# A two-layer encoder on one core: the next layer's loads issued behind operand loads of w_ffn_out, and PSUM buffers of its own for the last of seven products

## The chip, the cores and the metric

The kernel runs on one core of one Trainium2 chip. The metric is the device time of one launch in microseconds. Before the change three runs took 2110.39, 2110.87 and 2112.12 us; the median is 2110.87.

The engines are called by their names in the profile: PE (TensorE, matrix products into PSUM), PEld (its weight loads), DVE (VectorE), ACT (ScalarE), POOL (GpSimd) and SP (SyncE, whose queue issues nearly all DMAs of this kernel). Each runs its own instructions in order and waits for others by semaphores.

## The reference

Two layers over x of 1024 tokens by 1024 channels, all float32:

```python
for l in range(DEPTH):                                    # DEPTH = 2
    h = _rmsnorm(x, g_pre_mix[l])
    z = h @ w_in[l]
    zf, zq, zk, zv, zm = jnp.split(z, splits, axis=-1)
    y_f = _fourier_mix(zf, w_fourier[l])
    ...                                                   # y_a: windowed attention of zq, zk, zv
    mkv = _rmsnorm(mem, g_mem[l]) @ w_mem_kv[l]           # mem: 256 rows by 1024
    km, vm = jnp.split(mkv, 2, axis=-1)
    y_m = _memory_attn(zm.reshape(b, s, N_MEM_HEADS, HEAD_DIM), km, vm)
    ...                                                   # x = x + norm(concat(y_f, y_a, y_m) @ w_out[l])
    ...                                                   # gate, up = norm(x) @ w_ffn_in[l]; width 2816 each
    ...                                                   # x = x + norm((silu(gate) * up) @ w_ffn_out[l])
```

The memory projection `mkv` depends on inputs alone, so the kernel can make that of layer 1 at any time while layer 0 runs.

## The kernel before, in words

**Precision.** Every matrix product of float32 operands is made as three products of high and low halves: `split` (ACT L151 copies the high half, DVE L152 subtracts it to get the low half) makes `hi` and `lo`, and PE adds hi x hi, hi x lo and lo x hi.

**Stages.** A layer is mixing (projections, Fourier, windowed and memory attention, output projection), then `ffn_in` (product with w_ffn_in, silu and gate), then `ffn_out` (product with w_ffn_out). Both parts of the FFN work by Strassen's scheme: of each matrix cut into two by two quarters, seven products of sums of quarters instead of eight. `ffn_in` writes the seven sums of gated quarters to DRAM (`actd`, L1193), 11 tiles of 128 x 512 for each product.

**`ffn_out`** (L1255) runs the products in the order 5, 3, 4, 1, 7, 2, 6. A product has 11 steps k. For each, `out_sums` (L1229) loads a tile of `actd` (L1233) and splits it, loads one or two blocks of w_ffn_out (L1239), adds or subtracts these on DVE (L1251) and splits the result. Then `step` (L1270) issues three matmuls of 128x128 by 128x512 for each of four row blocks p: 12 a step, 132 a product. The raw tiles live in rings of 3 (`ras`) and 6 (`rbs`) buffers, the split operands in a ring `abs_` of 6 buffers in layer 0 and 15 in layer 1. The last product of layer 1 (`late`) runs row blocks 0 and 1 over all k first, and blocks 2 and 3 after them.

**PSUM.** The four results of a product (`fo`) are in four PSUM tags `pd`, `av`, `sc`, `pT`, with two buffers each, which they share with everything else on PE. Products 5, 4, 1 and 2 take new buffers. Products 3, 7 and 6 add to the PSUM tiles of the product ahead of them (`new` is false), so that the first matmul of 6 on a tile follows the reading of product 2's result from it (L1307). After each product its tiles are added to the four quarters of the output, `c11` to `c22`, by ACT copies or DVE TENSOR_TENSORs (L1293 to L1309).

**The next layer's loads.** In layer 0, `after(i)` (L1446) is called behind each product. Behind product 5 it emits `mem.make()` for layer 1: two loads of `mem` rows (L427, 512 KB each), g_mem (L216), eight loads of w_mem_kv (L356, 256 KB each) with their splits, the transposes `mTp` on PE (L439), and the products `kmp` and `vmp` (L162; 192 matmuls in all), which take PSUM buffers of tag `pT`. Behind product 1 it emits `zf_load()` and `fourier_tables(28)`: loads of parts of w_in for layer 1 (L356, L372), scaled by a gain on POOL (L342) or on ACT and DVE (L380) and split, and small Fourier tables (L498, L501). The rest of layer 1's beginning (`hTp`, `kvp`, `zT` on PE) mixes with products 2 and 6.

**Order.** The program is written in the order of the code, and the Tile scheduler then puts each engine's instructions in an order of its own by a simulated timeline: loads that wait for nothing may go far ahead of where they are written. `tc.issue_after(x)` is a scope whose DMAs stay behind the instruction x in that order; before, only the loads of the residual `x1d` (L1426) use it, with `lastld[0]`, the `actd` load that was written last.

Of the kernel before, what the change touches and what calls it, by code (L numbers as in the profile page):

```python
# [16 lines left out]
ALU = mybir.AluOpType  # L17
# [51 lines left out]
def tile_encoder(ctx: ExitStack, tc: tile.TileContext, T, C, out):  # L69
# [36 lines left out]
    def big(*shape, dt=F32R):  # L106

        return bp.tile([P, *shape], dt, tag="big", name=nm("big"))
# [34 lines left out]
    def ps(shape, name="ps", tag="pd"):  # L143
        return psp[tag].tile([P] + list(shape), F32, tag=tag, name=nm(name))
# [24 lines left out]
    def cst(*shape):  # L169
# [20 lines left out]
        out=mask[:, 0:P], in_=mask[:, 0:P], pattern=[[1, P]], compare_op=ALU.is_ge,  # L190
# [4 lines left out]
        out=mask[:, 2 * P : 3 * P], in_=mask[:, 2 * P : 3 * P], pattern=[[-1, P]],  # L195
# [988 lines left out]
    def up_out(q, g, actd, p):  # L1184

        V, G = nc.vector, nc.vector if p == NFF // 2 - 1 else nc.gpsimd
        a = [acts(512) for _ in range(4)]
        for i, c in enumerate(q.out):
            (G if i in (0, 3) else V).tensor_tensor(out=a[i], in0=c, in1=g[i], op=ALU.mult)  # L1189
        a11, a21, a12, a22 = a  # L1190

        def put(i, s):
            nc.sync.dma_start(actd[i - 1, p], s)  # L1193

        put(3, a11)
        put(4, a22)
        for i, x, y, eng in ((1, a11, a22, G), (2, a21, a22, V), (5, a11, a12, G)):
            s = acts(512)
            eng.tensor_tensor(out=s, in0=x, in1=y, op=ALU.add)
            put(i, s)  # L1200
        V.tensor_tensor(out=a21, in0=a11, in1=a21, op=ALU.subtract)
        put(6, a21)
        G.tensor_tensor(out=a12, in0=a12, in1=a22, op=ALU.subtract)
        put(7, a12)
# [22 lines left out]
    lastld = [None]  # L1227

    def out_sums(l, actd, i, k):  # L1229

        ab = abs_(2, 2, 512, dt=F32R)
        raw = ras(512)
        lastld[0] = nc.sync.dma_start(raw, actd[i - 1, k])  # L1233
        split(ab[:, 0, 0], ab[:, 0, 1], raw)

        def block(r, c):
            w = rbs(512)
            r0 = (2 * k + r) * P
            nc.sync.dma_start(w, T["w_ffn_out"][l, r0 : r0 + P, c * 512 : c * 512 + 512])  # L1239
            return w  # L1240

        if i in (2, 5):
            s = block(i == 5, i == 5)
        else:
            x, y, op = {
                4: ((1, 0), (0, 0), ALU.subtract), 3: ((0, 1), (1, 1), ALU.subtract), 1: ((0, 0), (1, 1), ALU.add),
                7: ((1, 0), (1, 1), ALU.add), 6: ((0, 0), (0, 1), ALU.add),
            }[i]
            x, y = block(*x), block(*y)
            s = bsums(512)  # L1250
            nc.vector.tensor_tensor(out=s, in0=x, in1=y, op=op)  # L1251
        split(ab[:, 1, 0], ab[:, 1, 1], s)
        return ab

    def ffn_out(l, actd, load, out, after, half, late):  # L1255

        n = NFF // 2  # L1260
        fb = [big(2, D, dt=F32) for _ in range(4)]
        rows = [fb[t // 2][:, t % 2] for t in range(NT)]
        c11, c12, c21, c22 = ([rows[4 * r + p][:, c * 512 : c * 512 + 512] for p in range(4)] for r in range(2) for c in range(2))
        add, sub = ALU.add, ALU.subtract
        TT = nc.vector.tensor_tensor

        def step(pt, p, ab, first, last, new):
            sl = slice(p * P, p * P + P)
            for j, (x, y) in enumerate(((0, 0), (0, 1), (1, 0))):
                mm(pt, ab[:, 0, x, sl], ab[:, 1, y], start=new and first and j == 0, stop=last and j == 2, skip_group_check=not new)  # L1270

        for i in (5, 3, 4, 1, 7, 2, 6):
            new = i in (5, 4, 1, 2)
            if new:
                pts = [ps([512], "fo", ("pd", "av", "sc", "pT")[p]) for p in range(4)]
            whole = 2 if i == 6 and late else 4
            ops = []
            for k in range(n):
                ops.append(out_sums(l, actd, i, k))
                for p in range(whole):  # L1280
                    step(pts[p], p, ops[k], k == 0, k == n - 1, new)
                t = {(2, 2): 0, (2, 7): 1, (6, 1): 2, (6, 5): 3}.get((i, k))
                if t is not None:
                    load(t)
                    out(t, rows[t])
                if i == 6 and k in (7, 8, 9, 10):
                    load(k - 3)
            for p in range(4):
                pt = pts[p]
                if p >= whole:  # L1290
                    for k in range(n):
                        step(pt, p, ops[k], k == 0, k == n - 1, new)
                if i == 5:  # L1293
                    nc.scalar.copy(c22[p], pt)
                    nc.scalar.copy(c11[p], pt)
                if i == 3:
                    nc.scalar.copy(c12[p], pt)
                    TT(out=c22[p], in0=pt, in1=c22[p], op=sub)
                if i == 4:
                    nc.scalar.copy(c21[p], pt)  # L1300
                    TT(out=c11[p], in0=c21[p], in1=c11[p], op=sub)
                if i == 1:
                    TT(out=c22[p], in0=pt, in1=c22[p], op=add)
                if i == 7:
                    TT(out=c11[p], in0=pt, in1=c11[p], op=add)
                if i == 2:
                    TT(out=c21[p], in0=pt, in1=c21[p], op=add)  # L1307
                if i == 6:
                    TT(out=c22[p], in0=c22[p], in1=pt, op=sub)  # L1309
                    if late:  # L1310
                        out(4 + p, rows[4 + p])
            after(i)
        if not late:
            for t in range(4, NT):
                out(t, rows[t])
                if t == 5:
                    half()
# [25 lines left out]
    mem = Memory(0, 32, 80, 20, 16, "pd")  # L1343
    mix = Mix(0, hT, mem)
# [13 lines left out]
    for l in range(DEPTH):  # L1358
# [58 lines left out]
        if l + 1 < DEPTH:  # L1417
            mem = Memory(l + 1, 16, 0, 16, 28, "pT")
            mix = Mix(l + 1, nhT, mem)
# [26 lines left out]
        def after(i):  # L1446
            if last:
                return
            if i == 5:
                mem.make()  # L1450
            if i == 1:
                mix.zf_load()
                mix.fourier_tables(28)

        xs_.i, xs_.ks = 0, (36, 24, 12, 16, 20, 28, 0) if last else (36, 24, 28, 20, 36, 24, 28, 46)
        ffn_out(l, actd, last_x, last_tile, after, lambda: mix.zf(0), last)
        if not last:
            norm_T(st.pop(NT - 1), nhT, NT - 1, "av")
# [43 lines left out]
```

## Time and profile before

| what | us |
|---|---|
| median of three runs | 2110.87 |
| the profiled execution | 2111.43 |
| its span | 2109.6 |
| mean granted clock of PE in it | 0.978 |
| layer 0, `ffn_out`, first to last matmul | 829.09 to 1075.8 |
| layer 1, `ffn_out`, first to last matmul | 1875.04 to 2101.1 |

The span is the profiled part of the execution. The lines of the profile are read like this: a row of the timeline has a start, a length, engine, line, operation and tiles; a bracket gives the idle time of the engine ahead of it and the instruction whose end released it. "x12" counts instructions that stand together. A row's matmuls overlap, so their length is that of the row and not twelve times a mean. All that the argument needs is shown where it is used.

### The profile page before, as it was taken

How to read it: one execution, taken by the hardware profiler on the slowest of the kernel's cores; microseconds unless marked ns; L12 is line 12 of the kernel's file. 1: busy time of each engine (PE TensorE's matmuls, PEld its weight loads, DVE VectorE, ACT ScalarE, POOL GpSimd, SP SyncE). 2: the span in 40 equal slices, each digit the busy share in tenths (PEclk: the TensorE clock that was granted, in tenths of full speed). 3: DMA queues.
4: the chain of work that ended last, by engine and by line, in shares of the span. 5: the costliest groups of instructions: out<-in, count | busy, mean ns of one | idle time of the engine just before them, and what ended most of it. 6: DMA issues, size and time to landing. Idle time of an engine off the chain costs nothing.

```text
span 2109.6 us, 28534 instructions
## 1 busy us (share of the span) xinstructions
PE 2004.4 (95%) x9587; PEld 1650.9 (78%) x9587; DVE 1576.5 (75%) x2532; ACT 1068.9 (51%) x2270; POOL 715.0 (34%) x819
## 2 busy tenths in 40 slices
PE   7998999799999999999999979997999999999997
PEld 6876887588888887788788758775788888878885
DVE  5668757887877877686856786679887787778774
ACT  7467767643333334444545676776333333345441
POOL 5345436343434334100523544453342343400021
PEclk9999999899999999999999989998999999999998
DMA  6112123423323326787821112233232232379872
GB/s 218 42 51 66 69 92 116 144 75 104 111 95 108 107 86 224 279 280 262 285 92 44 45 65 86 78 133 115 85 130 95 95 110 95 112 234 332 298 270 102
DMA packets 173347, 286.48 MB, mean 136 GB/s; under 512 B 15464, under 2 KB 73360, under 8 KB 173200
## 3 DMA queue, kind: packets, MB, share of 16 engines
q1 hardware_dynamic: 165136, 265.78, 37.7%
q10 hardware_dynamic: 8064, 18.88, 2.3%
q8 instruction: 75, 1.23, 0.2%
q14 instruction: 72, 0.59, 0.1%
HBM read 218.02 MB, written 66.58 MB: 135 GB/s over the span
## 4 chain that ended last, share of the span: by engine, by line
PE 77%; DVE 7%; DMA 6%; ACT 5%; issue 3%; POOL 2%; SPq 0%; DVEq 0%; ACTq 0%; POOLq 0%
PE fo L1270 15%; PE qz L1137 10%; PE qy L1137 10%; PE qx L1137 10%; PE mo L162 7%; PE qw L1137 5%; PE kvp L162 4%; DVE arena_r L152 3%; PE qp L162 3%; PE zT L162 2%; DMA arena_f<-actd 2%; PE pT L798 2%; PE sc L761 2%; ACT arena_r L151 1%; DMA arena_f<-in_w_ffn_out 1%
## 5 line engine op out<-in xcount | busy, mean ns | idle before, releaser
L151 ACT CAST arena_r<-arena_f 128x512 fp32r<-128x512 f32 (+2 forms) x780 | 443.8, 591 | 653.6 <-PE qz L1137 116.4
L152 DVE TENSOR_TENSOR arena_r<-arena_f,arena_r 128x512 fp32r<-128x512 f32 (+1 forms) x676 | 506.8, 770 | 154.4 <-ACT arena_r L151 151.6
L1270 PE MATMUL fo<-arena_r 128*128 128x512 f32 x1848 | 433.7, 396 | 22.8 <-ACT arena_r L151 12.7
L1270 PEld LDWEIGHTS fo<-arena_r 128*128 128x128 f32 x1848 | 351.7, 191 | 100.2 <-ACT arena_r L151 15.0
L1137 PE MATMUL qy<-arena_r 128*128 128x512 f32 x1056 | 263.6, 399 | 20.6 <-ACT arena_r L151 12.4
L1137 PEld LDWEIGHTS qy<-arena_r 128*128 128x128 f32 x1056 | 202.7, 193 | 65.6 <-ACT arena_r L151 13.0
L1127 DVE TENSOR_TENSOR arena_f<-arena_f 128x512 f32<-128x512 f32 x220 | 205.8, 939 | 8.9 <-issue 2.4
L1137 PE MATMUL qz<-arena_r 128*128 128x512 f32 x704 | 196.6, 389 | 1.2 <-DVE arena_r L152 1.2
L1157 POOL TENSOR_TENSOR arena_f<-arena_f 128x512 f32<-128x512 f32 x44 | 74.3, 1688 | 311.2 <-ACT arena_f L1142 311.2
L1137 PEld LDWEIGHTS qz<-arena_r 128*128 128x128 f32 x704 | 132.1, 188 | 29.0 <-DVE arena_r L152 1.6
L210 POOL TENSOR_SCALAR rrsv<-rss 128x1 f32<-128x1 f32 x32 | 13.1, 410 | 396.8 <-ACT arena_f L323 218.1
L152 POOL TENSOR_TENSOR arena_r<-arena_f,arena_r 128x256 fp32r<-128x256 f32 (+2 forms) x104 | 85.1, 823 | 129.6 <-ACT arena_r L151 100.5
L1137 PE MATMUL qx<-big,arena_r 128*128 128x512 f32 x528 | 127.1, 389 | 1.7 <-ACT arena_f L1142 1.7
L1137 PE MATMUL qx<-arena_r 128*128 128x512 f32 x528 | 127.9, 389 | 0.5 <-ACT arena_r L151 0.5
L1137 PE MATMUL qw<-arena_r 128*128 128x512 f32 x528 | 128.3, 389 | 0.0
L1189 POOL TENSOR_TENSOR arena_f<-arena_f 128x512 f32<-128x512 f32 x40 | 66.7, 1667 | 159.7 <-DVE arena_f L1169 122.4
L1137 PEld LDWEIGHTS qx<-big,arena_r 128*128 128x128 f32 x528 | 99.0, 188 | 22.6 <-ACT arena_f L1142 2.1
L1137 PEld LDWEIGHTS qx<-arena_r 128*128 128x128 f32 x528 | 99.1, 188 | 21.4 <-ACT arena_r L151 0.9
L1137 PE MATMUL qz<-big,arena_r 128*128 128x512 f32 x352 | 115.6, 389 | 0.0
L1137 PEld LDWEIGHTS qw<-arena_r 128*128 128x128 f32 x528 | 99.1, 188 | 20.7
L162 PE MATMUL mo<-big,arena_r 128*128 128x512 f32 x384 | 102.7, 408 | 0.5 <-ACT arena_f L1001 0.5
L162 PE MATMUL mo<-arena_r 128*128 128x512 f32 x384 | 101.9, 403 | 0.5 <-ACT arena_f L1001 0.5
(227 smaller groups left out, 3516.1 us busy)
## 6 DMA issues: line engine op xcount, KB each, us to landing
arena_f<-in_w_ffn_out SPq DMA_DIRECT2D x264, 256.0 KB, 4.3
arena_f<-in_w_ffn_in SPq DMA_DIRECT2D x88, 512.0 KB, 3.7
actd<-arena_f SPq DMA_DIRECT2D x154, 256.0 KB, 3.7
arena_f<-actd SPq DMA_DIRECT2D x154, 256.0 KB, 4.1
arena_f<-in_w_in SPq DMA_DIRECT2D x40, 256.0 KB, 2.8
arena_f<-in_x SPq DMA_DIRECT2D x16, 512.0 KB, 5.3
arena_f<-in_w_out SPq DMA_DIRECT2D x32, 256.0 KB, 2.7
pmd<-arena_f ACTq DMA_DIRECT2D x32, 256.0 KB, 2.0
```

The costliest lines, as they stand in the source:

```text
L151: nc.scalar.copy(hi, src)
L152: return (lo_eng or nc.vector).tensor_tensor(out=lo, in0=src, in1=f32(hi), op=ALU.subtract)
L162: mm(self.dst, a, b, start=self.i == 0, stop=self.i == self.n - 1)
L210: nc.gpsimd.tensor_scalar(out=v, in0=ss, scalar1=1.0 / n, scalar2=EPS, op0=ALU.mult, op1=ALU.add)
L761: mm(pt, lhs, self.kst[g][i][:, k0 * P : k1 * P], start=i == 0, stop=i == 1)
L798: nc.tensor.transpose(pT[:, h, :], es_[h // 2][:, h % 2, j * P : j * P + P], ident)
L1127: nc.vector.tensor_tensor(out=s, in0=a, in1=b, op=op)
L1137: mm(pt, a, b, start=start and n == 0, stop=n == 11, skip_group_check=not start)
L1157: nc.gpsimd.tensor_tensor(out=self.v, in0=self.v, in1=self.s2, op=ALU.add)
L1189: (G if i in (0, 3) else V).tensor_tensor(out=a[i], in0=c, in1=g[i], op=ALU.mult)
L1270: mm(pt, ab[:, 0, x, sl], ab[:, 1, y], start=new and first and j == 0, stop=last and j == 2, skip_group_check=not new)
```

## The change

The loads of `after(i)` stand in an `issue_after` scope behind the last `actd` load of product i, and the memory projection moves from behind product 5 to behind product 3. Product 6 takes new PSUM buffers, as products 5, 4, 1 and 2 do. Since product 6 no longer adds to product 2's result, that result is added to `c21` and also subtracted from `c22` when product 2 ends (four more TENSOR_TENSORs a layer, L1308 after), and product 6 is added to `c22` with the sign of its operand turned (L1201).

```diff
-        V.tensor_tensor(out=a21, in0=a11, in1=a21, op=ALU.subtract)
+        V.tensor_tensor(out=a21, in0=a21, in1=a11, op=ALU.subtract)
         put(6, a21)
...
         for i in (5, 3, 4, 1, 7, 2, 6):
-            new = i in (5, 4, 1, 2)
+            new = i not in (3, 7)
             if new:
                 pts = [ps([512], "fo", ("pd", "av", "sc", "pT")[p]) for p in range(4)]
...
                 if i == 2:
                     TT(out=c21[p], in0=pt, in1=c21[p], op=add)
+                    TT(out=c22[p], in0=c22[p], in1=pt, op=sub)
                 if i == 6:
-                    TT(out=c22[p], in0=c22[p], in1=pt, op=sub)
+                    TT(out=c22[p], in0=pt, in1=c22[p], op=add)
...
         def after(i):
             if last:
                 return
-            if i == 5:
-                mem.make()
-            if i == 1:
-                mix.zf_load()
-                mix.fourier_tables(28)
+            with tc.issue_after(lastld[0].ins):
+                if i == 3:
+                    mem.make()
+                if i == 1:
+                    mix.zf_load()
+                    mix.fourier_tables(28)
```

The scheduler turns this into another order on every engine. From L1308 on, lines after are one higher than before, and from L1450 on two.

**SP, first operand loads of product 5 in layer 0**, before: between the loads of `actd` and w_ffn_out stand pieces of w_mem_kv and w_in.

```order
L356 DMA arena_f<-in_w_mem_kv 128x2x256
L1239 DMA arena_f<-in_w_ffn_out 128x512
L356 DMA arena_f<-in_w_mem_kv 128x2x256
L1233 DMA arena_f<-actd 128x512
L1239 DMA arena_f<-in_w_ffn_out 128x512 x2
L1233 DMA arena_f<-actd 128x512
L356 DMA arena_f<-in_w_in 128x2x256
L356 DMA arena_f<-in_w_mem_kv 128x2x256
L356 DMA arena_f<-in_w_in 128x2x256
L1233 DMA arena_f<-actd 128x512
```

After, the same loads begin behind the last `actd` load of product 3 (the second of the x2 in the first row here).

```order
L1233 DMA arena_f<-actd 128x512 x2
L427 DMA arena_f<-in_mem 128x1024 x2
L356 DMA arena_f<-in_w_mem_kv 128x4x128 x3
L216 DMA arena_f<-in_g_mem 128x1024
L1233 DMA arena_f<-actd 128x512 x2
L1239 DMA arena_f<-in_w_ffn_out 128x512 x3
L1233 DMA arena_f<-actd 128x512
L1239 DMA arena_f<-in_w_ffn_out 128x512 x3
L356 DMA arena_f<-in_w_mem_kv 128x4x128
```

The rest of w_mem_kv follows among product 4's loads, and the pieces of w_in stand behind the last `actd` load of product 1.

**PE, where the memory projection stands in layer 0.** After, fo_7032 to fo_7035 are products 5 and 3, and fo_7644 to fo_7647 product 4. The first rows are the end of product 3 and the start of product 4:

```order
L1270 MATMUL fo_7034<-arena_r 128x512 x3
L1270 MATMUL fo_7035<-arena_r 128x512 x3
L439 MATMUL mTp_7504<-const,arena_f 128x128 x4
L439 MATMUL mTp_7511<-const,arena_f 128x128 x4
L1270 MATMUL fo_7644<-arena_r 128x512 x3
L1270 MATMUL fo_7645<-arena_r 128x512 x3
```

and these are the projection and what follows it in product 4:

```order
L162 MATMUL kmp_7539<-arena_r 128x256 x23
L162 MATMUL kmp_7565<-arena_r 128x256 x24
L162 MATMUL vmp_7591<-arena_r 128x256 x24
L162 MATMUL vmp_7617<-arena_r 128x256 x24
L1270 MATMUL fo_7647<-arena_r 128x512 x18
L1270 MATMUL fo_7644<-arena_r 128x512
```

Before, mTp stood in the last steps of product 5 and the first of product 3, and kmp and vmp behind that; now they stand behind product 3 and inside product 4, whose fourth row block (fo_7647) makes up its first six steps, 18 matmuls, after vmp.

**DVE, the step from product 2 to product 6 in layer 0.** Before, the eviction of product 2 (L1307) mixes with operand sums (L1251) and splits (L152) of product 6 and work of layer 1:

```order
L152 TENSOR_TENSOR arena_r<-arena_f,arena_r 128x512
L1307 TENSOR_TENSOR big_7030<-fo_8376,big_7030 128x512
L1251 TENSOR_TENSOR arena_f<-arena_f 128x512
L152 TENSOR_TENSOR arena_r<-arena_f,arena_r 128x512
L1307 TENSOR_TENSOR big_7030<-fo_8377,big_7030 128x512
L1251 TENSOR_TENSOR arena_f<-arena_f 128x512
L1307 TENSOR_TENSOR big_7031<-fo_8378,big_7031 128x512
```

After, each L1307 has an L1308 behind it that reads the same PSUM tile:

```order
L152 TENSOR_TENSOR arena_r<-arena_f,arena_r 128x512
L1307 TENSOR_TENSOR big_7030<-fo_8376,big_7030 128x512
L1308 TENSOR_TENSOR big_7030<-big_7030,fo_8376 128x512
L1251 TENSOR_TENSOR arena_f<-arena_f 128x512
L152 TENSOR_TENSOR arena_r<-arena_f,arena_r 128x512
L1307 TENSOR_TENSOR big_7030<-fo_8377,big_7030 128x512
L1308 TENSOR_TENSOR big_7030<-big_7030,fo_8377 128x512
L1307 TENSOR_TENSOR big_7031<-fo_8378,big_7031 128x512
L1308 TENSOR_TENSOR big_7031<-big_7031,fo_8378 128x512
```

The sums and splits behind them move back by as many instructions; on PE, product 6 writes to tiles of its own and no row of it refers to fo_8376 to fo_8379 any more. In layer 1 the eight evictions stand together, behind all splits of product 6.

## The prediction

> **What bounds the kernel now.** I read the page first: busy times, slices, the chain.
>
> ```profile
> PE 2004.4 (95%) x9587; PEld 1650.9 (78%) x9587; DVE 1576.5 (75%) x2532; ACT 1068.9 (51%) x2270; POOL 715.0 (34%) x819
> ...
> PE   7998999799999999999999979997999999999997
> ...
> PE 77%; DVE 7%; DMA 6%; ACT 5%; issue 3%; POOL 2%; SPq 0%; DVEq 0%; ACTq 0%; POOLq 0%
> ```
>
> PE is busy 95% of 2109.6 us and is 77% of the chain. The change takes no matmul away, so only PE's idle time and slow clock can pay. What touches the change are the two runs of `ffn_out`, 826 to 1076 us and 1874 to 2110 us. PE's waits in the first, summed by releaser:
>
> ```profile
> PE fo L1270 <- ACT arena_r L151: 7.6, 4, 3.4
> PE fo L1270 <- DVE big L1307: 3.7, 1, 3.7
> PE fo L1270 <- ACT big L1295: 0.8, 1, 0.8
> ```
>
> The timeline of PE says where these are and, in brackets, what ended each (columns: start, length, operation, idle time before). Layer 0's start, its step from product 2 to 6, layer 1's start, and its step from 2 to 6:
>
> ```profile
> 829.09 2.88 PE L1270 MATMUL fo<-arena_r 128*128 128x512 f32 x12
> 835.36 9.92 PE L1270 MATMUL fo<-arena_r 128*128 128x512 f32 x36 [3.38 <-ACT arena_r L151]
> 847.06 8.45 PE L1270 MATMUL fo<-arena_r 128*128 128x512 f32 x36 [1.78 <-ACT arena_r L151]
> 856.78 8.45 PE L1270 MATMUL fo<-arena_r 128*128 128x512 f32 x36 [1.27 <-ACT arena_r L151]
> 866.40 2.12 PE L1270 MATMUL fo<-arena_r 128*128 128x512 f32 x8 [1.17 <-ACT arena_r L151]
> 868.36 1.03 PE L439 MATMUL mTp<-const,arena_f 128*128 128x128 f32 x8
> 869.15 1.17 PE L1270 MATMUL fo<-arena_r 128*128 128x512 f32 x4
> ...
> 1035.88 1.66 PE L162 MATMUL kvp<-big,arena_r 128*128 128x512 f32 x6 [0.51 <-DVE arena_r L152]
> 1041.21 11.95 PE L1270 MATMUL fo<-arena_r 128*128 128x512 f32 x40 [3.67 <-DVE big L1307]
> ...
> 1875.04 5.60 PE L1270 MATMUL fo<-arena_r 128*128 128x512 f32 x24
> 1885.73 119.22 PE L1270 MATMUL fo<-arena_r 128*128 128x512 f32 x516 [5.09 <-ACT arena_r L151]
> 2005.50 57.41 PE L1270 MATMUL fo<-arena_r 128*128 128x512 f32 x252 [0.55 <-DVE big L1303]
> 2068.03 33.07 PE L1270 MATMUL fo<-arena_r 128*128 128x512 f32 x132 [5.12 <-DVE big L1307]
> ```
>
> The price of a matmul comes from the long undisturbed row, 57.41 / 252 = 0.228 us, so a product of 132 is 30.1 us and a step k of 12 is 2.73 us. Product 5 of layer 0 runs from 829.09 to 870.32, which is 41.2 us; without its 30.1 and the 0.8 us of transposes (868.36 to 869.15) **10.3 us are lost**, 7.6 of them idle and the rest slow restarts (x36 took 9.92 instead of 8.2). At 1041.21 the loss is 3.67 + 0.5 idle and 11.95 - 40 x 0.228 = 2.8 of slow matmuls, **7.0**. At 2068.03 it is 5.12 + (33.07 - 30.1) = **8.1**. At 1885.73, where no loads for another layer exist, it is 5.09 + (119.22 - 117.6) = 6.7; that row is my warning against expecting all of the 10.3.
>
> Why a restart is slow, and what the DMA engines did, show the windows (busy time and count of PE, PEld, DVE, ACT, POOL, then granted clock, DMA share, GB/s):
>
> ```profile
> 830.00:840.00 10.00, 6.62 (x23) 5.03 (x22) 8.46 (x10) 4.69 (x9) 8.26 (x9) 0.83 0.92 302
> 850.00:860.00 10.00, 8.73 (x39) 6.91 (x38) 6.47 (x11) 3.42 (x6) 0.00 (x0) 1.00 1.03 382
> 890.00:900.00 10.00, 10.00 (x57) 8.73 (x57) 3.98 (x6) 3.03 (x6) 0.00 (x0) 1.00 0.49 168
> ...
> 1041.00:1050.00 9.00, 8.79 (x27) 7.10 (x28) 9.00 (x12) 3.41 (x6) 5.07 (x4) 0.68 0.98 364
> ...
> 1436.87:1456.87 20.00, 12.63 (x33) 9.44 (x34) 19.04 (x28) 9.75 (x18) 4.37 (x5) 0.51 0.54 179
> ...
> 2060.00:2080.00 20.00, 14.88 (x53) 11.68 (x52) 9.68 (x17) 3.04 (x5) 0.00 (x0) 0.83 0.33 119
> ```
>
> The clock fell to 0.83, 0.68 and 0.83 around the stalls of over 3 us. In product 5 the DMA engines are full (0.92 to 1.03); past 890 us they are half idle (0.49).
>
> **The change, part by part.** *Start of layer 0.* The chain of waits, in order of time, runs there through the loads that the change moves:
>
> ```profile
> 836.47 5.95 DMA arena_f<-in_w_in
> 842.42 0.09 issue
> 842.51 2.81 POOL arena_f L342 x2
> ...
> 845.87 1.14 ACT arena_r L151 x2
> 847.01 0.04 issue
> 847.06 8.47 PE fo L1270 x36
> ```
>
> PE waited at 847.06 for an ACT split, ACT (which runs in order) stood behind the conversion of a piece of w_in by POOL, and that behind its 5.95 us load. In the order of after, all of in_mem, w_mem_kv and w_in stand behind the 11th actd load of product 3 or 1 on SP; what is left ahead of product 5 on SP, ACT and POOL belongs to product 5. What is late next is the actd load of an early k, whose slot is given back by the last gate of `ffn_in`; in layer 1 the same thing costs 6.7. So the gain lies between 10.3 - 6.7 = 3.6 and 10.3. I take **-9.4** (about 1 us of stall left), nearer the upper end, because layer 0's own rows before 835.36 end in conversions of w_in and not in that slot.
>
> *The memory projection behind product 3.* Two in_mem loads were issued and transposed at these rows (SP issue; PE consumed them at 868.36):
>
> ```profile
> 851.83 0.33 SPq L427 DMA_DIRECT2D arena_f<-in_mem  x1
> ...
> 853.82 0.33 SPq L427 DMA_DIRECT2D arena_f<-in_mem  x1
> ```
>
> So issue to mTp took 868.36 - 851.83 = 16.5 us. In after, mTp stands behind the last row of product 3 on PE, at 829.1 + 1 + 2 x 30.1 = 890.3. The actd load ahead of in_mem takes a ring slot that k7's split gives back, and that split needs a buffer that PE gives back after k1, at 860.2 + 2 x 2.73 = 865.7; with two more steps for ACT and DVE I take 871. Then mTp is ready at 887.5, 2.8 us before PE comes to it. Queued behind it on PE is product 4; its first six k run on three row blocks, because the fourth PSUM buffer is the one that kmp and vmp hold, and 18 matmuls catch up: order, not work. Cost between nothing (DMA share 0.49 there, DVE 3.98 of 10) and 10.3 (all that these loads cost where they stood): I take **+1.0**, near the lower end because of that half-idle window.
>
> *The step from product 2 to 6, layer 0.* PE need not wait for L1307 any more, but four TENSOR_TENSORs are added behind it on DVE:
>
> ```profile
> 1040.47 0.68 DVE L1307 TENSOR_TENSOR big<-fo,big 128x512 f32<-128x512 f32 x1
> ...
> 1052.94 1.90 DVE L152 TENSOR_TENSOR arena_r<-arena_f,arena_r 128x512 fp32r<-128x512 f32 x3 [1.66 <-ACT arena_r L151]
> ...
> 2065.40 1.88 DVE L152 TENSOR_TENSOR arena_r<-arena_f,arena_r 128x512 fp32r<-128x512 f32 x3
> 2067.21 2.47 DVE L1307 TENSOR_TENSOR big<-fo,big 128x512 f32<-128x512 f32 x4
> ```
>
> Four cost 2.47 us (last row). DVE is full at 1041 to 1050 (9.00 of 9.00) and first idle at 1052.94. PE begins 3.67 us earlier and DVE's splits end 2.47 later, so 6.1 us of operand lead are asked for; whether it is there no row shows. With all of it the gain is 7.0; with none, PE stalls 6.1 and restarts slowly for 2.8, 8.9 against 7.0, a loss of 1.9. Following after's rows on DVE with the durations of before, the sixth operand's split ends some 17.8 us after product 2, and PE wants it at 14 (five steps of 2.73 and a transpose), an estimate; 3.8 late with a restart of 2.3 makes 6.1: **-0.9**, between the ends.
>
> *The same step in layer 1.* All splits of product 6 are done by 2067.28, and PE would start at 2005.50 + 57.41 = 2062.9 and, with two row blocks first (6 matmuls, 1.37 us a step), come to its tenth operand at 2075.2. DVE's work is 8 us ahead; the four added adds come behind every split. The whole loss goes: **-8.1**. The clock part of it can be weighed: rows show 1.7 lost after 3.38 idle, 2.8 after 3.67, 1.6 after 5.09 and 3.0 after 5.12. [...]
>
> *Everything between.* The scheduler gives another order to layer 1's mixing, with the same instructions. Its price is bounded by two orders of the same work, from the first qp row to the first row of `ffn_out`:
>
> ```profile
> 139.42 2.79 PE L162 MATMUL qp<-big,arena_r 128*128 128x512 f32 x11 [2.19 <-ACT arena_f L584]
> ...
> 1176.71 3.58 PE L162 MATMUL qp<-big,arena_r 128*128 128x512 f32 x15
> ```
>
> 829.09 - 139.42 = 689.7 and 1875.04 - 1176.71 = 698.3: 8.7 us to either side. I take 0.
>
> Layer 1's own start keeps its 6.7. **Sum:** -9.4 + 1.0 - 0.9 + 0 - 8.1 = -17.4. The profiled execution took 2111.43 us (0.56 above the median of 2110.87), so 2094.0 there and 2093.5 as a median.
>
> **The rivals.**
> *The start stalls as in layer 1.* Removing the loads only uncovers the slot: gain 3.6 instead of 9.4, 2099.3. For it speaks 1885.73, the same code without the loads; against it, that layer 0's stalls end in conversions of w_in.
> *The loss moves with the loads.* Product 4 pays 10.3 instead of 1.0: 2102.8. For it: same bytes, same engines in order; against it, 0.49 of DMA.
> *Operands take the place of the PSUM wait in layer 1.* If the splits slip by 8 us, the 8.1 are not gained: 2101.6. Against it, all splits were done at 2067.28. [...]
> *Slower: the memory rows come late.* mTp blocks PE in order. If the in_mem issue waits until product 3 ends (the actd load ahead of it is on the same queue), PE idles 16.5 us and restarts at 0.51 of the clock (the 1436.87 row: 20 x 0.49 = 9.8 lost): 26.3 instead of 1.0, 2118.8. It decides from an issue at some 887, where 13 us idle and 9.8 of clock eat the gain and the 4.2 us of 0.2%; I put it at 871.
> *No change.* The start as in layer 1, and the loss moved: -3.6 + 10.3 - 0.9 - 8.1 = -2.3, 2108.6; or the new order of mixing costs 8.7 on top of a rival.
>
> **How the numbers follow.** Forecast 0.49; start as in layer 1 0.22; loss moved 0.13; operands in the tail 0.05; no change 0.06; memory late 0.05. About 0.2%, 4.2 us, is what a measurement of this kernel can tell from no change. Faster 0.86 (the first four, less 0.03 where the mixing adds to them), same 0.08, slower 0.06. The range takes the forecast with 8.7 to the good side and the three faster rivals with some of it to the other: 2084 to 2106.
>
> **What would show it.** Right: in product 5 of layer 0 no PE wait over 1.5 us and 31 us in all; mTp behind product 3 with under 1 us of idle; L1308 eight times at some 0.68 us; in layer 1 no idle time between product 2 and 6, and the last 132 matmuls in 30 us; in layer 0 a DVE or ACT wait of some 4 us in the middle of product 6 in place of the one ahead of it. Wrong: a wait of 4 us for an actd split at the start; waits with "ACT arena_r" inside product 4; a long wait ahead of mTp; a layer 1 mixing that is several us longer or shorter for no instruction more.

## The result, and the profile after

Four runs of the kernel after took 2088.43 to 2097.46 us, median 2089.91; four of the kernel before 2110.39 to 2112.96, median 2111.49. The ratio is 0.9906, 95% interval 0.989 to 0.9922. The profiled execution of after took 2091.0 us with a span of 2089.2, against 2111.43 and 2109.6 before: 20.4 us less. The forecast was 17.4 less.

The page of after, busy times and chain:

```profile
PE 1994.7 (95%) x9587; PEld 1646.5 (79%) x9587; DVE 1578.8 (76%) x2540; ACT 1069.9 (51%) x2270; POOL 713.1 (34%) x819
...
PE 74%; DVE 9%; DMA 7%; ACT 5%; issue 3%; POOL 2%; SPq 0%; DVEq 0%; ACTq 0%; POOLq 0%
```

PE has the same 9587 matmuls, DVE eight instructions more (2540 for 2532). The waits of PE in the two runs of `ffn_out`, first 820 to 1070 us and then 1850 to 2095 us (us in total, times, longest):

```profile
PE fo L1270 <- ACT arena_r L151: 1.9, 1, 1.9
PE hTp L314 <- DVE arena_r L152: 1.4, 1, 1.4
PE fo L1270 <- ACT big L1295: 0.7, 1, 0.7
PE fo L1270 <- DVE arena_r L152: 0.5, 1, 0.5
...
PE fo L1270 <- ACT arena_r L151: 5.4, 1, 5.4
PE fo L1270 <- DVE big L1303: 0.2, 1, 0.2
```

No wait on L1307 is left in either. The 7.6 us for ACT's splits in product 5 of layer 0 are gone; the one of 1.9 is new and stands elsewhere, at the start of product 7 (971.18 below). Layer 1's 5.1 have become 5.4. The timeline of PE shows the places:

```profile
834.48 30.24 PE L1270 MATMUL fo<-arena_r 128*128 128x512 f32 x132
865.44 30.26 PE L1270 MATMUL fo<-arena_r 128*128 128x512 f32 x132 [0.72 <-ACT big L1295]
895.54 1.03 PE L439 MATMUL mTp<-const,arena_f 128*128 128x128 f32 x8
...
971.18 9.56 PE L1270 MATMUL fo<-arena_r 128*128 128x512 f32 x41 [1.87 <-ACT arena_r L151]
...
1032.77 0.66 PE L314 MATMUL hTp<-const,arena_f 128*128 128x128 f32 x4 [1.40 <-DVE arena_r L152]
1033.18 11.39 PE L1270 MATMUL fo<-arena_r 128*128 128x512 f32 x49
...
1049.19 5.29 PE L1270 MATMUL fo<-arena_r 128*128 128x512 f32 x22 [0.51 <-DVE arena_r L152]
...
1863.54 5.60 PE L1270 MATMUL fo<-arena_r 128*128 128x512 f32 x24
1874.55 118.58 PE L1270 MATMUL fo<-arena_r 128*128 128x512 f32 x516 [5.41 <-ACT arena_r L151]
1993.31 87.35 PE L1270 MATMUL fo<-arena_r 128*128 128x512 f32 x384 [0.18 <-DVE big L1303]
```

Product 5 of layer 0 is one row of 132 matmuls in 30.24 us, where it had been 41.2 in six pieces. Products 2 and 6 of layer 1 are part of one row of 384, where 5.12 us of idle time had stood between them.

Cut at the first and the last matmul of each `ffn_out`, the two spans stand so (us; each is a difference of two starts or ends in the timeline of PE):

| stage | before | after | difference |
|---|---|---|---|
| up to `ffn_out` of layer 0 | 829.1 | 834.5 | +5.4 |
| `ffn_out` of layer 0 | 246.8 | 232.1 | -14.7 |
| layer 1 up to its `ffn_out` | 799.1 | 797.0 | -2.1 |
| `ffn_out` of layer 1 | 226.1 | 217.1 | -9.0 |
| after the last matmul | 8.5 | 8.5 | 0 |

The first row is a loss that nothing in the change explains: PE, ACT, DVE and POOL run the same instructions in the same order at least until 814 us of the kernel before, and the first `qy` row of PE (L1137) already stands at 394.51 us before and at 399.76 after. It is taken up with the experiments.

Not all of the 14.7 us is saved work or waiting. Before, six `kvp` matmuls and one more group of four `hTp` transposes stood inside layer 0's `ffn_out`, some 1.7 us by their rows; after, they stand behind it.

### The profile page after: what moved, and what is told of

Same layout as the page of the kernel before. It is cut to its first block, busy times and chain, and to the rows that moved or that the text cites. A ratio compares the mean times of both kernels' runs of the same rounds, so it can differ in the third digit from the quotient of the medians.

```text
span 2089.2 us, 28535 instructions
## 1 busy us (share of the span) xinstructions
PE 1994.7 (95%) x9587; PEld 1646.5 (79%) x9587; DVE 1578.8 (76%) x2540; ACT 1069.9 (51%) x2270; POOL 713.1 (34%) x819
## 4 chain that ended last, share of the span: by engine, by line
PE 74%; DVE 9%; DMA 7%; ACT 5%; issue 3%; POOL 2%; SPq 0%; DVEq 0%; ACTq 0%; POOLq 0%
PE fo L1270 13%; PE qx L1137 11%; PE qy L1137 10%; PE qz L1137 10%; PE mo L162 7%; PE qw L1137 5%; PE kvp L162 4%; DVE arena_r L152 3%; PE qp L162 3%; DMA arena_f<-actd 3%; PE zT L162 2%; PE pT L798 1%; ACT arena_r L151 1%; DMA arena_f<-in_w_ffn_out 1%; PE sc L761 1%
## 5 line engine op out<-in xcount | busy, mean ns | idle before, releaser
L151 ACT CAST arena_r<-arena_f 128x512 fp32r<-128x512 f32 (+1 forms) x780 | 443.7, 591 | 632.6 <-PE qz L1137 119.9
L152 DVE TENSOR_TENSOR arena_r<-arena_f,arena_r 128x512 fp32r<-128x512 f32 (+1 forms) x676 | 509.4, 774 | 148.1 <-ACT arena_r L151 136.8
L1270 PE MATMUL fo<-arena_r 128*128 128x512 f32 x1848 | 425.1, 391 | 8.7 <-ACT arena_r L151 7.3
L1270 PEld LDWEIGHTS fo<-arena_r 128*128 128x128 f32 x1848 | 346.6, 188 | 82.4 <-ACT arena_r L151 8.1
L1137 PE MATMUL qy<-arena_r 128*128 128x512 f32 x1056 | 261.9, 397 | 22.3 <-ACT arena_r L151 12.5
L1137 PEld LDWEIGHTS qy<-arena_r 128*128 128x128 f32 x1056 | 201.7, 192 | 66.6 <-ACT arena_r L151 13.3
L1137 PE MATMUL qz<-arena_r 128*128 128x512 f32 x704 | 196.6, 389 | 1.1 <-DVE arena_r L152 1.1
L1137 PEld LDWEIGHTS qz<-arena_r 128*128 128x128 f32 x704 | 132.1, 188 | 28.9 <-DVE arena_r L152 1.5
L152 POOL TENSOR_TENSOR arena_r<-arena_f,arena_r 128x256 fp32r<-128x256 f32 (+2 forms) x104 | 87.0, 842 | 129.5 <-ACT arena_r L151 84.4
L1137 PE MATMUL qx<-big,arena_r 128*128 128x512 f32 x528 | 127.1, 389 | 1.7 <-ACT arena_f L1142 1.7
L1137 PE MATMUL qx<-arena_r 128*128 128x512 f32 x528 | 127.9, 389 | 0.5 <-ACT arena_r L151 0.5
L1137 PE MATMUL qw<-arena_r 128*128 128x512 f32 x528 | 128.3, 389 | 0.0
L1137 PEld LDWEIGHTS qx<-big,arena_r 128*128 128x128 f32 x528 | 99.0, 188 | 22.6 <-ACT arena_f L1142 2.1
L1137 PEld LDWEIGHTS qx<-arena_r 128*128 128x128 f32 x528 | 99.1, 188 | 21.4 <-ACT arena_r L151 0.9
L1137 PE MATMUL qz<-big,arena_r 128*128 128x512 f32 x352 | 115.7, 389 | 0.0
L1137 PEld LDWEIGHTS qw<-arena_r 128*128 128x128 f32 x528 | 99.1, 188 | 20.6
L162 PE MATMUL mo<-big,arena_r 128*128 128x512 f32 x384 | 102.2, 406 | 0.8 <-ACT arena_f L1001 0.8
L162 PE MATMUL mo<-arena_r 128*128 128x512 f32 x384 | 100.7, 403 | 0.9 <-POOL arena_r L152 0.6
```

The lines of the kernel that those rows point to most:

```text
L151: nc.scalar.copy(hi, src)
L152: return (lo_eng or nc.vector).tensor_tensor(out=lo, in0=src, in1=f32(hi), op=ALU.subtract)
L162: mm(self.dst, a, b, start=self.i == 0, stop=self.i == self.n - 1)
L1137: mm(pt, a, b, start=start and n == 0, stop=n == 11, skip_group_check=not start)
```

## The experiments

All times are medians; "above" and "under" compare with 2089.91 for the kernel after, or with the run of it that stood beside them. The comparison with before has its interval. Beside the time I read the same five stages from each profile, because the time of one kernel moves by several us from run to run (the kernel before took 2103.95 to 2116.96 in the last group).

**The PSUM part alone.** The change without this piece, the loads as before:

```diff
-            with tc.issue_after(lastld[0].ins):
-                if i == 3:
-                    mem.make()
-                if i == 1:
-                    mix.zf_load()
-                    mix.fourier_tables(28)
+            if i == 5:
+                mem.make()
+            if i == 1:
+                mix.zf_load()
+                mix.fourier_tables(28)
```

> The change's PSUM part alone (own PSUM buffers for product 6, turned sign, the four added TENSOR_TENSORs a layer); the next layer's loads as before. My theory: the two parts are independent. Layer 1's step from product 2 to 6 gains 8 to 9 us, layer 0's about 5 us, and the start of layer 0's ffn_out loses its 10 us as before: about 14 us under before, ratio 0.9935. Rival: layer 0's step gains nothing without the moved loads, because DVE's backlog there is what remains: 8 to 9 us under before, ratio 0.996, with a DVE or ACT wait of about 4 us inside product 6.

2095.79 us, ratio 0.9924 (0.9911 to 0.9938): 16.3 under before. `ffn_out` took 239.9 us in layer 0 (6.9 less than before, of which 1.7 is the `kvp` and `hTp` work that moved out as in the kernel after) and 217.0 in layer 1 (9.1 less). Product 5 still stalls; PE's timeline of this run:

```profile
830.40 2.88 PE L1270 MATMUL fo<-arena_r 128*128 128x512 f32 x12
837.46 18.96 PE L1270 MATMUL fo<-arena_r 128*128 128x512 f32 x72 [4.18 <-ACT arena_r L151]
```

The rival falls: layer 0's step gains without the moved loads, and its 6.9 less 1.7 is the 5 us that I gave it.

**The load part alone.** The kernel before with the other half of the change:

```diff
-            if i == 5:
-                mem.make()
-            if i == 1:
...
+            with tc.issue_after(lastld[0].ins):
+                if i == 3:
+                    mem.make()
+                if i == 1:
...
```

> The change's load part alone (issue_after scope, memory projection behind product 3); product 6 adds to product 2's PSUM tiles as before. My theory: product 5 of layer 0 runs in about 31 us instead of 41 and nothing comes back later: about 10 us under before, ratio 0.995. Rival: the gain at layer 0's step from 2 to 6 comes from the moved loads and not from PSUM: about 15 us under before, ratio 0.993.

2103.14 us, ratio 0.9958 (0.9944 to 0.9971): 8.9 under before. Layer 0's `ffn_out` took 238.1 us, 8.7 less than before, and layer 1's 226.4, the same. The step in layer 1, PE's timeline of this run:

```profile
2061.94 31.75 PE L1270 MATMUL fo<-arena_r 128*128 128x512 f32 x132 [7.14 <-DVE big L1307]
```

16.3 and 8.9 add up to 25.2, where the whole gave 21.6; the sums of the stages, 6.9 + 8.7 = 15.6 in layer 0 and 9.1 - 0.4 = 8.7 in layer 1, meet the 14.7 and 9.0 of the table. By the stages the parts are independent to within 1 us; in the profiled execution of the whole, what is missing lies in front of the stages that they touch.

**The scope behind product 5 instead of 3.**

```diff
             with tc.issue_after(lastld[0].ins):
-                if i == 3:
+                if i == 5:
                     mem.make()
```

> The kernel after, with the memory projection back behind product 5 but still in the scope, so that its loads stand behind the last actd load of product 5. My theory: it is the place on SP's queue behind product 5's own loads that counts, and product 3 has room: within 3 us of the kernel after. Rival: the loss moves with the loads into product 3, whose DMA windows were 0.8 to 1.0 busy: 8 to 10 us above the kernel after, with ACT arena_r waits inside product 3.

2090.92 us, ratio 0.9905 (0.9888 to 0.9922): the same as the kernel after; layer 0's `ffn_out` 230.6 us, without a PE wait of over 0.4 us in products 5, 3 and 4. The rival falls. One product later or earlier is worth nothing here.

**Behind product 3, but without the scope.**

```diff
-            with tc.issue_after(lastld[0].ins):
-                if i == 3:
-                    mem.make()
-                if i == 1:
...
+            if i == 3:
+                mem.make()
+            if i == 1:
...
```

> The kernel after without the issue_after scope: the memory projection is written behind product 3, but its loads and those of w_in may be issued early again. My theory: SP's queue is then as before the change, product 5 takes 41 us again, and only the PSUM part gains: 14 us under before, ratio 0.9935, equal to the run with the PSUM part alone. Rival: that the projection's splits and transposes stand later on ACT and PE is what frees product 5: about 21 us under before, equal to the kernel after.

2098.31 us, ratio 0.9938 (0.9924 to 0.9952): 2.5 above the PSUM part alone and not equal to it; in their profiles that difference lies in front of layer 0's `ffn_out` and between the two stages. SP's rows for these loads are those of before, and product 5 has its four waits again (3.10, 0.94, 1.27 and 1.17 us, 238.8 us in all). So the place in the written program counted for nothing for these loads, which wait for nothing: the scope does all of it.

**Own PSUM buffers in layer 1 only.**

```diff
-            new = i not in (3, 7)
+            new = i not in ((3, 7) if late else (3, 7, 6))
...
                 if i == 2:
                     TT(out=c21[p], in0=pt, in1=c21[p], op=add)
-                    TT(out=c22[p], in0=c22[p], in1=pt, op=sub)
+                    if late:
+                        TT(out=c22[p], in0=c22[p], in1=pt, op=sub)
...
```

(with the sign of a21 and of product 6's addition as before in layer 0).

> The kernel after, with product 6 of layer 0 adding to product 2's PSUM tiles again as before the change (no L1308 there); layer 1 keeps its own PSUM buffers. My theory: layer 0's step from product 2 to 6 is worth about 5 us by itself (idle 3.7 and a slow restart against 1.9 of short waits): 4 to 7 us above the kernel after, with the wait on DVE L1307 of 3 us or more back in layer 0. Rival, as I had forecast: the added adds eat it, and the time is within 2 us of the kernel after.

2094.75 us, ratio 0.9918 (0.9899 to 0.9937), 4.8 above after; layer 0's `ffn_out` 239.2 us, 7.2 above. Its step (lines are one higher in this kernel):

```profile
1033.07 1.53 PE L162 MATMUL kvp<-big,arena_r 128*128 128x512 f32 x6
1038.13 10.99 PE L1271 MATMUL fo<-arena_r 128*128 128x512 f32 x40 [3.53 <-DVE big L1308]
```

Idle 3.5, then 10.99 us for 40 matmuls where 40 x 0.228 = 9.1; the 1.5 us of kvp that PE takes in between are work that stands behind product 6 in the kernel after. Without that and one `hTp` group, 7.2 is 5.5. My forecast of 0.9 falls.

**Which loads hold up product 5?** Only w_in and the tables in the scope:

```diff
-            with tc.issue_after(lastld[0].ins):
-                if i == 3:
-                    mem.make()
-                if i == 1:
+            if i == 5:
+                mem.make()
+            if i == 1:
+                with tc.issue_after(lastld[0].ins):
...
```

> The kernel after, with only w_in's loads and the Fourier tables in the scope; the memory projection is behind product 5 and unscoped as before, so that mem, g_mem and w_mem_kv (3.5 MB) stand among product 5's first loads again, and w_in does not. My theory, from the chain of waits that ran through POOL's conversion of w_in: most of the 10 us goes with w_in, 2 to 4 us remain; 2 to 4 us above the kernel after. Rival: it is the bytes on the DMA engines that hold up product 5, whoever they are for, and two thirds of them are mem's: 6 to 8 us above the kernel after.

2092.3 us, ratio 0.9902 (0.988 to 0.9923); layer 0's `ffn_out` 235.0 us, 3.0 above after. PE's timeline of product 5:

```profile
833.83 2.88 PE L1270 MATMUL fo<-arena_r 128*128 128x512 f32 x12
839.66 29.11 PE L1270 MATMUL fo<-arena_r 128*128 128x512 f32 x120 [2.94 <-ACT arena_r L151]
```

One wait of 2.9 us is left, and product 5 takes 34.9 us: 4.7 of the 10.3 are left and 5.6 went with w_in. So the three later waits went with w_in, which is a third of the bytes in all. That alone doesn't settle bytes against work, because all of w_mem_kv goes out ahead of product 5 (805.93 to 831.27); of what the kernel before issues for layer 1 within product 5, w_in is 1.25 of 2.75 MB. The windows of this run say more (columns as in the prediction):

```profile
840.00:850.00 10.00, 10.00 (x38) 8.09 (x37) 7.82 (x13) 3.50 (x7) 0.00 (x0) 0.83 0.95 299
850.00:860.00 10.00, 10.00 (x46) 8.27 (x45) 6.47 (x10) 4.21 (x8) 0.00 (x0) 1.00 0.98 374
```

The DMA engines are 0.95 and 0.98 busy under a PE at 10.00 of 10.00, and POOL, 5.79 us busy from 840 to 850 before, does nothing. So nearly full DMA engines alone did not hold up product 5. What is left is the work on the pieces of w_in, POOL's scaling and the ACT splits that queue behind it, as in the chain of the prediction. That split of the loss is shown; that this work is the cause is likely and not shown by itself, since w_in's bytes and its splits on ACT and DVE went with POOL's part.

**Only the memory projection in the scope.**

```diff
-            with tc.issue_after(lastld[0].ins):
-                if i == 3:
+            if i == 3:
+                with tc.issue_after(lastld[0].ins):
                     mem.make()
-                if i == 1:
-                    mix.zf_load()
+            if i == 1:
+                mix.zf_load()
...
```

> The kernel after, with only the memory projection in the scope. The raw buffers of w_in's pieces come from the same small ring as w_mem_kv's and after them, so w_in's loads can only follow w_mem_kv's: they stand among product 4's loads. My theory: the first scope alone keeps the start of product 5 clean, and product 4 has its operands far enough ahead: within 3 us of the kernel after. Rival: w_in's conversions on POOL, ACT and DVE next to mem's bring the stalls back in product 4: 5 us or more above it, with ACT arena_r waits there.

2086.44 us, ratio 0.9875 (0.9853 to 0.9897), 3.5 under after, though the intervals overlap; layer 0's `ffn_out` 228.3 us, 3.8 under. Its start is as clean as it can be, products 5 and 3 in one row:

```profile
829.22 60.35 PE L1270 MATMUL fo<-arena_r 128*128 128x512 f32 x264
```

The 1.87 us wait at 971.18 is also gone. In the kernel after, the chain of waits leads to it like this:

```profile
957.34 4.35 DMA arena_f<-c_chan
961.69 0.05 issue
961.74 1.78 DVE arena_f L1251
...
970.54 0.63 ACT arena_r L151
971.16 0.01 issue
971.18 3.89 PE fo L1270 x16
```

DVE's operand sum took 1.78 us beside POOL's splits of w_in (958.28 to 962.97), where it takes 0.69 with POOL idle (941.76). This wait is a cost of the second scope: at the start of product 7 one of 1.8 to 3.1 us stands in the profile of every run that has w_in's loads and the tables in the scope (eight with the kernel after), and in none of the six others. Without the scope w_in's first seven loads and the tables go out at 892 to 922 us in this run, in product 4, where PE waits 0.4 us; with it they go out at 949 to 971. Whether w_in's conversions or the tables make the wait, no run separates.

**Other raw slots in layer 1.**

```diff
+        if last:
+            ras.i, ras.ks = 0, (44, 40, 4, 6, 42)
```

> The kernel after, with another ring of raw actd tiles in layer 1's ffn_out: five slots that begin with ones that the last gates of ffn_in don't use, instead of three of which one is held until its last gate. My theory: layer 1's wait of 5.4 us behind the first two steps is for that slot and goes, with the slow restart behind it: 5 to 7 us under the kernel after, near 2084 us. Rival: the DMA engines are full there (0.93 to 1.02 before the change) and the wait comes back a step or two later: within 2 us of the kernel after.

2088.14 us, ratio 0.9887 (0.9867 to 0.9907): 1.8 under after, and layer 1's `ffn_out` 215.8 us, 1.3 less. PE's timeline at its start:

```profile
1860.31 11.04 PE L1270 MATMUL fo<-arena_r 128*128 128x512 f32 x48
1871.52 19.34 PE L1270 MATMUL fo<-arena_r 128*128 128x512 f32 x84 [0.16 <-ACT arena_r L151]
1893.69 26.59 PE L1270 MATMUL fo<-arena_r 128*128 128x512 f32 x109 [2.84 <-ACT big L1295]
```

The 5.4 us behind the first 24 matmuls are gone, so it was the slot. But half comes back between products 5 and 3, where ACT, which does the splits in order, reaches the copies of product 5 2.8 us late. The 1.3 us are no gain either: layer 1's `ffn_out` took 215.7 us in the repetition of the kernel after and 214.7 in the run ahead, both with the old slots. The rival holds.

**The last group: after again, two of these edits at once, a smaller ring, and the earlier scope.**

> The kernel after, unchanged, beside the next three on the same chip, so that they can be compared with it: 2088 to 2092 us. In front of layer 0's ffn_out it should differ from its first profile by some us (there the same order of instructions reached ffn_out 5.4 us later than in the kernel before), which is what I take for run-to-run differences.

2089.46 us, 0.9889 (0.9867 to 0.991). The same kernel reached layer 0's `ffn_out` at 828.5 us, 6.0 earlier than in its first profile; the stages behind took 232.1, 797.1 and 215.7.

Only the projection in the scope, and the raw slots:

> Two changes to the kernel after at once: only the memory projection in the scope (w_in's loads follow it through their common raw ring), and the five raw slots for actd tiles in layer 1. My theory: they are at different places and add up: 3 to 4 us from the first and 1 to 2 us from the second, 4 to 6 us under the kernel after. Rival: what the first showed was run-to-run difference, and the sum is within 2 us of the kernel after.

2084.71 us, 0.9864 (0.984 to 0.9889), 4.8 under the run beside it. The time is as forecast, but the stages don't show the sum: in the profiled execution, the slowest of the five (2088.73), layer 0's `ffn_out` took 230.9 us, 1.2 under, and layer 1's 216.7, 1.0 above. The wait at product 7 is gone there too; 1.9 us for ACT's copies between products 5 and 3 stand in its place, where the run above with the same layer 0 had none. So this wait, too, differs from run to run.

Four instead of six buffers of split operands in layer 0:

```diff
-        abs_.ks = (64, 72, 80, 88, 16, 24, 0, 8, 32, 40, 48, 56, 96, 104, 112) if last else (80, 88, 48, 56, 96, 104)
+        abs_.ks = (64, 72, 80, 88, 16, 24, 0, 8, 32, 40, 48, 56, 96, 104, 112) if last else (80, 88, 48, 56)
```

> The kernel after, with four instead of six buffers of split operands in layer 0's ffn_out. It asks why the moved loads cost nothing in product 4 although they fill the DMA engines there to 1.0 and more. My theory: six buffers and three raw tiles hold some 16 us of operands ahead of PE at that place, which product 5 at its start can't have; with four the loads show as ACT or DVE waits in products 3 and 4 of 5 us or more together, and layer 0's ffn_out takes 5 to 15 us longer. Rival: the lead is not needed, the engines are just fast enough there: products 3 and 4 stay without waits, and the time is within 2 us of the kernel after.

2101.4 us, 0.9948 (0.9927 to 0.9968), 11.9 above. Layer 0's `ffn_out` took 247.1 us, 15.0 more, of which 1.7 are `kvp` and `hTp` work of layer 1 that moved into it (the stage behind is 4.7 shorter). But the place is not the forecast one. PE's timeline in product 4 and in product 6:

```profile
908.97 0.96 PE L1270 MATMUL fo<-arena_r 128*128 128x512 f32 x3 [1.11 <-DVE arena_r L152]
...
1061.73 0.80 PE L1270 MATMUL fo<-arena_r 128*128 128x512 f32 x1 [2.96 <-ACT arena_r L151]
```

Products 3 and 4 wait 1.5 us together, not 5 or more; the rest is at the start (3.2), at the tables (3.1) and at the step to product 6. SP's rows give the lead there: the last `actd` load of product 3 goes out at some 876 us in the kernel after (the second of the x2) and at 881.6 here, and PE ends product 3 at 895.7 and 898.0.

```profile
874.89 1.53 SPq L1233 DMA_DIRECT2D arena_f<-actd  x2
...
881.63 0.36 SPq L1233 DMA_DIRECT2D arena_f<-actd  x1
```

Less the last step of 2.73 that is some 17 us of lead with six buffers and 13.7 with four. So two buffers are worth some 3 us of lead there, and 13.7 were still nearly enough for the loads; that lead is what makes them free is not shown by this, and the one forecast that would have borne it out, 5 us of waits in products 3 and 4, failed.

The projection behind product 5, alone in the scope, with the raw slots:

> The run before last but with the memory projection scoped behind product 5 instead of 3 (w_in's loads follow it), and the five raw slots in layer 1. My theory: one product earlier than product 4 there is less lead, but the scope at product 5 cost nothing before: within 2 us of the run with the scope behind product 3 and the same slots, 4 to 6 us under the kernel after. Rival: with w_in's conversions now in product 3 as well, waits come up there: 3 us or more above that run.

2083.39 us, 0.9864 (0.9841 to 0.9887), 6.1 under after beside it, and no different from the one with the scope behind product 3. It is the fastest median of the study. By the intervals no version is clearly apart from the kernel after, whose own interval in this group begins at 0.9867; what speaks for a gain is layer 0's `ffn_out`, 227.9 us against 232.1, and that the wait at product 7 is gone in all three runs without the second scope. Layer 1's took 215.9, so the raw slots show no part in it.

## Why the prediction came out right, point by point

*Start of layer 0: 9.4 forecast, 10.2 found.* Product 5 took 30.24 us, with nothing left of the 10.3. The load part alone gave 8.9 in all. The rival that layer 1's slot would show up here fell in every run with the scope on both groups and six split buffers; with four, 3.2 us stand there. In layer 1 itself the raw-slot run showed that it was that slot.

*The memory projection: 1.0 forecast, none found.* The transposes follow product 3 at 895.54 without a wait, and no PE wait stands until 971. The loads did go where the DMA engines then had nothing left (windows of after; PE, PEld, DVE, ACT, POOL, clock, DMA share, GB/s):

```profile
880.00:890.00 10.00, 10.00 (x46) 8.29 (x45) 8.43 (x13) 6.02 (x11) 1.73 (x4) 1.00 1.04 360
890.00:900.00 10.00, 10.00 (x50) 8.38 (x49) 9.59 (x17) 8.74 (x17) 0.00 (x0) 1.00 1.07 372
900.00:910.00 10.00, 10.00 (x51) 8.31 (x51) 8.29 (x14) 3.14 (x6) 0.00 (x0) 1.00 1.02 341
```

My reason, a half idle window of 0.49, was therefore none: the same full DMA engines that stood over product 5's stalls stand here over a PE at 10.00 of 10.00. The slower rival needed in_mem issued at 887; it went out at 876.5, which is 871.1 on the clock of before, where `ffn_out` starts 5.4 us earlier: my 871.

*w_in's loads behind product 1: no term, some 2 found.* The sum priced the new place of the projection's loads and not that of w_in's and the tables'. They cost the 1.87 us at 971.18, the wait of the second scope.

*The step from product 2 to 6 in layer 0: 0.9 forecast, some 5 found* (6.9 and 7.2 by the two runs, less the 1.7 of moved work). This is the term that was mis-sized. Only the size was off: PE and DVE do race for the sixth operand. I had its split 17.8 us after product 2 with PE there at 14, 3.8 late and a slow restart. In the row that begins at 1033.18 the first four matmuls are still product 2's, so product 6 starts at some 1034.1, and it waits for an operand only at 1049.19, 15.1 us on, for 0.51. No slow restart follows (22 matmuls in 5.29 us where 22 x 0.228 = 5.0, at a granted clock of 1.00), and the wait of some 4 us in the middle of product 6, which I had named as a sign, did not come. DVE's rows in after show why it was earlier (start, length):

```profile
1037.36 0.68 DVE L1307 TENSOR_TENSOR big<-fo,big 128x512 f32<-128x512 f32 x1
1037.96 0.68 DVE L1308 TENSOR_TENSOR big<-big,fo 128x512 f32<-128x512 f32 x1
1038.55 2.72 DVE L1251 TENSOR_TENSOR arena_f<-arena_f 128x512 f32<-128x512 f32 x1
...
1046.59 1.28 DVE L1251 TENSOR_TENSOR arena_f<-arena_f 128x512 f32<-128x512 f32 x2
1047.79 0.74 DVE L380 SCALAR_TENSOR_TENSOR big<-arena_f,const,big 128x512 fp32r<-128x512 f32 x1
```

and in before, at the same place:

```profile
1042.87 2.50 DVE L1251 TENSOR_TENSOR arena_f<-arena_f 128x512 f32<-128x512 f32 x1
...
1048.90 1.78 DVE L380 SCALAR_TENSOR_TENSOR big<-arena_f,const,big 128x512 fp32r<-128x512 f32 x1
```

The adds cost 0.68 us each, as forecast. One sum took 2.72 in after, but those that I had priced at before's slow lengths took 0.64 and 0.74. The 1.40 us ahead of hTp at 1032.77 is a new wait at product 2's end. It ends with DVE's L152 that reads the first group's PSUM tile (1032.03, 0.68 long), so it is for a PSUM buffer and not for an operand, and it stands (0.7 to 1.6 us) in every other run with own buffers in layer 0 and six split buffers.

*The step in layer 1: 8.1 forecast, 9.0 found,* 9.1 with the PSUM part alone. What is lost behind the wait can be read again from the runs that kept it: 31.75 - 30.1 = 1.7 us after 7.14 idle, and 10.99 - 9.1 = 1.9 after 3.53. Two more rows, of layer 1's buffers alone at product 7 and of the load part alone at layer 0's step, show that the length of the idle time doesn't set it:

```profile
970.07 11.16 PE L1271 MATMUL fo<-arena_r 128*128 128x512 f32 x41 [2.00 <-ACT arena_r L151]
...
1039.37 9.37 PE L1270 MATMUL fo<-arena_r 128*128 128x512 f32 x40 [2.97 <-DVE big L1307]
```

The first lost 1.8 us after 2.00 idle, the second 0.3 after 2.97. In before, the row at 847.06 lost 0.2 after 1.78 idle, at a granted clock of 1.00 (847 to 855.5), and in after the one at 1874.55 lost 1.0 after 5.41, at 0.85 (1874.5 to 1884.5). So these rows and those of the prediction show 0.2 to 3.0 us, and no fixed price. The wait itself was for DVE's reading of PSUM (3.67 and 5.12 us on L1307 before), and taking it away in both layers gave 16.3 us.

*Everything between: 0 forecast, 2.1 less found;* over all runs that stage took 795.7 to 800.5 us, the small ring aside, and before's 799.1 lies among them, so that the 2.1 are not told from chance. A bound of 8.7 was wider than needed.

*What the sum didn't hold:* 5.4 us more in front of layer 0's `ffn_out`. The sum was made from one execution of before against another of after, and two executions of the same program differ by as much there. By stages alone the change is worth 14.7 + 2.1 + 9.0 = 25.8, the sum of its two parts alone is 25.2, and the medians of the two comparisons of the kernel after give 21.6 and 23.7. That the two profiled executions differ by 20.4, only 3.0 from the forecast, is in part luck: the 5.4 of chance in front, and the 2 us of the second scope, took back most of what the other stages gave beyond the forecast, the step in layer 0 above all.

## What to carry to other kernels

A load that waits for nothing was put by this scheduler far ahead of where it was written; if it competes with the first operands of a stage, whose buffers are still empty, tie it to one of that stage's own late loads. It need not be moved to an idle DMA window: in product 4 even a full one (1.07 and 1.02 from 890 to 910 us) cost nothing here. Each group of moved loads has to be priced at its new place, though (w_in's cost 2 us at product 7), and it is worth asking which engine works on the loaded tile (in product 5 the pieces that POOL, ACT and DVE had to scale cost 5.6 us, the rest 4.7). The accumulation into a PSUM tile that another engine reads first was a wait on that engine's queue here (3.67 and 5.12 us on DVE L1307); where the sum can be made at eviction, a few instructions of 0.68 us bought the whole of it.

## What the hardware showed that was not expected

Two executions of one program on the same order of instructions reached layer 0's `ffn_out` at 828.5 and 834.5 us. The granted clock of the first 50 us (1.00 in the profile of before, 0.90 in both of after) is not what decides it, for 828.5 had 0.90 as well:

```profile
0.00:50.00 50.00, 39.23 (x227) 34.38 (x228) 28.89 (x59) 34.39 (x68) 23.96 (x48) 0.90 0.66 215
...
0.00:50.00 50.00, 40.02 (x237) 35.48 (x238) 29.57 (x59) 35.37 (x71) 25.00 (x50) 0.90 0.67 217
```

(the first of after's first profile, the second of its repetition). The 6 us are there by 208.60 us against 202.67 (the first `mo` row, L162, in layer 0's mixing) and stay the same from there on. What makes them stays open; a change of a few us in such a kernel has to be read by stages.
